# Recurrence gates of a hybrid decoder block as 64-row products on two halves of the array

## The chip, the cores and the metric

The kernel runs on one core of a Trainium2 chip. The time is the device time of one execution in microseconds (us). The kernel before took 1090.16 us, the median of three runs (1089.74 to 1090.64). The engines are named as in the profile: PE is TensorE (PEld its weight loads), DVE is VectorE, ACT is ScalarE, POOL is GpSimd, SP is the queue that starts most transfers. Each of them works off its own queue of instructions; semaphores tie the queues together.

## The reference

One decoder layer over 512 positions of 1024 channels. Three mixers work on the same normed input, their results are gated and merged, and a SwiGLU block follows. The change touches only the third mixer, a recurrence with 16 heads of 64 channels:

```python
def rglru_mixer(xr, gate, conv_w, conv_b, w_a, b_a, w_x, b_x, lam):
    xc = lax.conv_general_dilated(xr, conv_w[:, None, :], ...) + conv_b
    xh = xc.reshape(B, S, RNN_HEADS, RNN_HEAD_DIM)
    r = jax.nn.sigmoid(jnp.einsum('bshi,hio->bsho', xh, w_a).reshape(B, S, RNN_WIDTH) + b_a)
    i = jax.nn.sigmoid(jnp.einsum('bshi,hio->bsho', xh, w_x).reshape(B, S, RNN_WIDTH) + b_x)
    log_a = -LRU_C * r.astype(jnp.float32) * jax.nn.softplus(-lam.astype(jnp.float32))
    a = jnp.exp(log_a)
    b_in = jnp.sqrt(-jnp.expm1(2.0 * log_a)) * (i * xc).astype(jnp.float32)
    _, h = lax.associative_scan(combine, (a, b_in), axis=1)
    return h.astype(xr.dtype) * jax.nn.gelu(gate)
```

Each head has its own 64x64 matrix for the gate r (w_a) and for the gate i (w_x).

## The kernel before

All large products are made of 128x512 products of TensorE, with the channels on the partitions and the 512 positions along the free side. For precision every float32 operand is split in two parts, hi and lo (`split`, L130: ScalarE writes hi, VectorE writes lo as the rest), and a product of two operands becomes three: hi with hi, hi with lo, lo with hi. A tile (`matrix`, `passes`, L263) is 128 output channels: 8 blocks of input channels times three products, 24 products into one bank of PSUM. Its weights come in units of 512 KB; `unit` (L252) hands out the next one and starts the load and the split of the unit two tiles further on, into one of three buffers each for hi and lo.

The recurrence is done in two batches of four tiles (128 channels, so two heads, each). For a tile, `xr_tile`:

- makes the 24 products and adds the convolution: ScalarE writes xc from the bank (L499), VectorE adds three shifted terms (L501);
- splits xc into ch and cl (L131 on ScalarE, L136 on VectorE);
- makes both gates: the two 64x64 matrices of a tile lie on the diagonal of a 128x128 block of `wab`, with zeros beside them, so one gate is three 128x128 products into a bank of the tag "tr" (L509). ScalarE applies the sigmoid for r (L511) and a tanh for i (L514), and VectorE forms (tanh + 1) xc (L515).

`wab` is loaded and split early by `load_wab`, four splits of 512 elements per partition. After a batch, `rec_batch` makes the decay: a tanh of r per tile (L523), one square root over the four tiles (L524), exponentials (L530), each function set with a table load ahead of it, and then VectorE's scan (L542). The tiles `rg_tile` make the branch that the result is multiplied with, `gate_tile` (L712 to L724) the gates of another mixer, and `cmp_tile` a projection for it.

The order of the work: generators yield between pieces, and `run` draws them in turn. A tile that yields a number (`yield 4`) is put aside and drawn again that many yields later, so that its gates come out between the products of the next tile. A scheduler then sets the order on each engine; `tc.issue_after` makes an instruction stand behind another one. Banks of PSUM with the tag "mm" (six) and "tr" (two) are handed out in rotation.

Of the kernel before, what the change touches and what calls it, by code (L numbers as in the profile page):

```python
# [25 lines left out]
F32R = mybir.dt.float32r  # L26
I32 = mybir.dt.int32
AF = mybir.ActivationFunctionType
OP = mybir.AluOpType
# [23 lines left out]
def hybrid_block(ctx: ExitStack, tc: tile.TileContext, A, out):  # L53
# [61 lines left out]
    def bank(tag):  # L115
        return psum[1].tile([128, S], F32, tag=tag, name=nm(tag), bufs=psum[2][tag])
# [13 lines left out]
    def split(src, hi, lo, lo_eng=None):  # L130
        res["hi"] = SC.activation(hi, src, AF.Copy)  # L131
        e = lo_eng or V
        if e is GP:
            GP.tensor_sub(lo, src, f32(hi))
        else:
            res["lo"] = V.tensor_sub(lo, src, f32(hi))  # L136
# [318 lines left out]


    wab = {}

    def start_wab():
        wab["raw"] = slab("wabr", tag="s1", shape=(2, NK, 128))  # L460
# [2 lines left out]

    def load_wab():
        raw = wab["raw"]
        hi = slab("wabh", F32R, "wab", (2, NK, 128), 48)
        lo = slab("wabl", F32R, "wab", (2, NK, 128), 48)
        wab["hi"], wab["lo"] = hi, lo
        for _ in range(4):
            yield  # L470
        for k in range(0, NK, 2):
            split(raw[:, :, k:k + 2], hi[:, :, k:k + 2], lo[:, :, k:k + 2])
            yield

    yc = {}
    rec = {}
# [11 lines left out]
    def xr_tile(b, c):  # L488
# [11 lines left out]
        for i in (1, 2, 3):  # L500
            res["cv"] = V.scalar_tensor_tensor(xc[:, i:], ps[:, :S - i], cw(3 - i), xc[:, i:], op0=OP.mult, op1=OP.add)  # L501
        yield
        ch, cl = row("ch", F32R), row("cl", F32R)
        split(xc, ch, cl)
        yield 4
        for g, dst in ((0, "R"), (1, "TI")):
            pg = bank("tr")
            for t, (w, x) in enumerate((("hi", ch), ("hi", cl), ("lo", ch))):
                PE.matmul(pg, wab[w][:, g, k, :], x, start=(t == 0), stop=(t == 2))  # L509
            if g == 0:  # L510
                SC.activation(rec[b]["R"][:, c, :], pg, AF.Sigmoid, bias=vec[:, V_BA + k:V_BA + k + 1])  # L511
            else:
                ti = rec[b]["TI"][:, c, :]
                last = SC.activation(ti, pg, AF.Tanh, scale=0.5, bias=half[:, 0, k:k + 1])  # L514
                res["ti"] = last, V.scalar_tensor_tensor(ti, ti, 1.0, xc, op0=OP.add, op1=OP.mult)  # L515
            yield

    def rec_batch(b):
        r = rec[b]
        r["T"] = slab("t", tag="s2")  # L520
        for c in range(4):
            k = 4 * b + c
            SC.activation(r["T"][:, c, :], r["R"][:, c, :], AF.Tanh, scale=sp4[:, k:k + 1])  # L523
        root = SC.activation(r["T"], r["T"], AF.Sqrt, scale=1.0 / 16)  # L524

        def exps(cs):
# [1739 lines left out]
```

## Time and profile before

| | us |
|---|---|
| median of three runs | 1090.16 |
| the profiled execution | 1089.44 |
| its span, first to last instruction | 1087.7 |
| PE busy | 1078.3 |
| DVE busy | 883.0 |
| ACT busy | 661.7 |
| gate products (L509), first to last start | 66.8 to 143.6 |

The profile is of one execution. A row of a timeline has the start and the length in us, the engine, the line, the operation, its output and inputs, and in brackets the idle time of the engine ahead of it and what ended it. A row of a group has the count, the busy time, the mean duration in ns and the idle time ahead. A row of stretches has the time from and to, its length, the busy time of each engine (PE, PEld, DVE, ACT, POOL) with the number of instructions, the granted clock of TensorE (1.00 is full speed) and the share and rate of the transfers. Recorded products of TensorE overlap, so their durations add up to more than the time that they take.

### The profile page before, as it was taken

To read this page: it belongs to the slowest core of one execution; us is meant where nothing else is said; L and a number is where in the kernel's file an instruction comes from. 1 tells how busy PE (TensorE), PEld (TensorE's weight loads), DVE (VectorE), ACT (ScalarE), POOL (GpSimd) and SP (SyncE) were. 2 spreads that over 40 slices of the span, in tenths; PEclk is the share of its full clock that TensorE was granted. 3 is DMA by queue.
4 is the path that set the end of the run, shared out by engine and by line. 5 is a ranking of instruction groups with operands and counts; after the bars stand their busy time and mean duration, and the time that the engine had idled before them with its cause. 6 is when DMAs were issued, how large, how long until landed. Compare 5 with 4: busy or idle time off the path is not lost.

```text
span 1087.7 us, 16765 instructions
## 1 busy us (share of the span) xinstructions
PE 1078.3 (99%) x6450; PEld 948.5 (87%) x6450; DVE 883.0 (81%) x1557; ACT 661.7 (61%) x1210; POOL 29.0 (3%) x41
## 2 busy tenths in 40 slices
PE   9999999999999999999999999999999999999997
PEld 7888888999889888898888889988999999998886
DVE  6967779669675899998998887876988888889675
ACT  6757574454444676876777655555666666667542
POOL 0000000000000000000000000000000000022200
PEclk9999999999999999999999999999999999999999
DMA  8332325430322221102111134271323322378902
GB/s 312 113 99 82 97 86 204 178 98 20 117 78 78 78 59 39 59 20 79 59 39 59 58 118 136 72 257 39 117 78 117 117 104 97 130 227 202 191 20 97
DMA packets 35312, 115.07 MB, mean 106 GB/s; under 512 B 3584, under 2 KB 3984, under 8 KB 34336
## 3 DMA queue, kind: packets, MB, share of 16 engines
q1 hardware_dynamic: 28496, 97.01, 27.0%
q0 software_dynamic: 5152, 11.09, 5.0%
q10 hardware_dynamic: 1584, 5.90, 1.4%
q8 instruction: 50, 0.82, 0.3%
q14 instruction: 30, 0.25, 0.1%
HBM read 111.89 MB, written 2.10 MB: 105 GB/s over the span
## 4 chain that ended last, share of the span: by engine, by line
PE 97%; DVE 1%; DMA 0%; issue 0%; ACT 0%; DVEq 0%; SPq 0%; ACTq 0%
PE mm L263 37%; PE mm L1755 18%; PE mm L1273 7%; PE mm L1894 6%; PE mm L625 4%; PE mm L1509 4%; PE o L992 4%; PE sc L954 3%; PE tr L979 3%; PE tr L1894 3%; PE mm L870 2%; PE tr L784 1%; PE tr L509 1%; PE mm L1611 1%; PE tr L685 1%; PE tr L892 1%
## 5 line engine op out<-in xcount | busy, mean ns | idle before, releaser
L263 PE MATMUL mm<-hh,hi 128*128 128x512 f32 x504 | 199.5, 396 | 0.0
L263 PE MATMUL mm<-hh,lo 128*128 128x512 f32 x504 | 197.4, 392 | 0.0
L263 PE MATMUL mm<-hl,hi 128*128 128x512 f32 x504 | 196.9, 391 | 0.0
L136 DVE TENSOR_TENSOR lo<-raw,hi 128x1024 fp32r<-128x1024 f32 (+1 forms) x105 | 121.0, 1153 | 38.4 <-ACT hi L131 35.3
L131 ACT ACTIVATE hi<-raw 128x1024 fp32r<-128x1024 f32 (+1 forms) x105 | 105.3, 1003 | 46.5 <-PE mm L263 17.3
L263 PEld LDWEIGHTS mm<-hh,lo 128*128 128x128 f32 x504 | 94.6, 188 | 19.7
L263 PEld LDWEIGHTS mm<-hl,hi 128*128 128x128 f32 x504 | 94.7, 188 | 18.4 <-issue 0.2
L263 PEld LDWEIGHTS mm<-hh,hi 128*128 128x128 f32 x504 | 94.7, 188 | 18.0 <-PE mm L1273 0.2
L960 ACT ACTIVATE P<-P,ast 128x128 f32<-128x128 f32 (+3 forms) x128 | 70.7, 555 | 23.1 <-DVE ast L958 22.5
L958 DVE CUSTOM_DVE_ANT_0 P<-sc,mask 128x128 f32<-128x128 f32 (+3 forms) x128 | 57.9, 484 | 8.2 <-PE sc L954 7.3
L131 ACT ACTIVATE ph<-tr 128x512 fp32r<-128x512 f32 x80 | 46.9, 592 | 25.9 <-PE tr L979 24.0
L136 DVE TENSOR_TENSOR pl<-tr,ph 128x512 fp32r<-128x512 f32 x80 | 54.4, 685 | 2.7 <-PE o L992 0.9
L954 PE MATMUL sc<-K,q 128*128 128x512 f32 (+2 forms) x192 | 51.0, 368 | 0.0
L1755 PE MATMUL mm<-t,hi 128*128 128x256 f32 x288 | 50.7, 276 | 0.0
L1894 PE MATMUL mm<-hi,u 128*128 128x512 f32 x160 | 50.1, 389 | 0.0
L979 PE MATMUL tr<-ident,P 128*128 128x128 f32 x320 | 48.7, 273 | 0.0
L979 PEld LDWEIGHTS tr<-ident,P 128*128 128x128 f32 x320 | 39.0, 140 | 9.8 <-DVE pl L136 1.0
L136 DVE TENSOR_TENSOR lo<-bs,hi 128x1024 fp32r<-128x1024 f32 x28 | 34.1, 1220 | 11.6 <-ACT hi L131 11.6
L1755 PEld LDWEIGHTS mm<-t,hi 128*128 128x128 f32 x288 | 43.4, 188 | 0.0
L1755 PE MATMUL mm<-fh,hi 128*128 128x256 f32 x144 | 40.0, 278 | 0.0
L1755 PE MATMUL mm<-fh,lo 128*128 128x256 f32 x144 | 39.8, 276 | 0.0
L1755 PE MATMUL mm<-fl,hi 128*128 128x256 f32 x144 | 39.8, 276 | 0.0
(489 smaller groups left out, 2896.6 us busy)
## 6 DMA issues: line engine op xcount, KB each, us to landing
raw<-in_w_in SPq DMA_DIRECT2D x64, 512.0 KB, 3.5
rawp<-in_w_fi SPq DMA_DIRECT2D x20, 1024.0 KB, 5.1
bs<-in_w_fo POOLq DMA_DIRECT2D x20, 512.0 KB, 8.1
raw<-in_w_br SPq DMA_DIRECT2D x14, 512.0 KB, 3.6
w<-in_cw ACTq DMA_DIRECT2D x4, 1024.0 KB, 6.7
raw<-in_w_o SPq DMA_DIRECT2D x8, 512.0 KB, 4.1
bs<-in_w_fo SPq DMA_DIRECT2D x8, 512.0 KB, 8.0
raw<-in_w_v SPq DMA_DIRECT2D x6, 512.0 KB, 4.9
```

The costliest lines, as they stand in the source:

```text
L131: res["hi"] = SC.activation(hi, src, AF.Copy)
L136: res["lo"] = V.tensor_sub(lo, src, f32(hi))
L263: res["mm"] = PE.matmul(ps[:m, n0:n1], w[:, k * 128:k * 128 + m], x[k][:, n0:n1], start=(t == 0), stop=(t == 3 * NK - 1))
L625: res["mm"] = PE.matmul(b[c], x[k][:, c * 128:(c + 1) * 128], w[:, kk * 512:kk * 512 + 512], start=(k == 0 and t == 0), stop=(k == NK - 1 ...
L954: PE.matmul(ps[:, :w * n].rearrange("p (b n) -> p b n", b=w), lhs, K[:, i, brs[0]:brs[-1] + 1, :n], start=(i == 0), stop=(i == 1))
L958: V.tensor_tensor_reduce(out=t, in0=ps[:, b * n:b * n + n], in1=mask[0][:, S - n:], scale=-0.125, scalar=3.0e38, op0=OP.add, op1=OP.min, a ...
L960: SC.activation(t, t, AF.Exp, scale=-1.0, bias=st[:, 0, j, b:b + 1], accum_out=st[:, 1, j, b:b + 1])
L979: PE.transpose(pt[:, j * 128:(j + 1) * 128], self.part(j, br)[:, kt * 128:(kt + 1) * 128], ident)
L992: PE.matmul(po, VV[:, kt, g % 2, br].rearrange("p i d -> p (i d)"), x, start=(br == 0 and kt == 0 and t == 0), stop=(br == 1 and kt == a a ...
L1273: res["mm"] = PE.matmul(ps, u[:, k * 128:k * 128 + 128], v[:, k], start=(start and k == t == 0), stop=(k == 3 and t == 2), skip_group_chec ...
L1755: res["mm"] = PE.matmul(ps, w[:, k * 128:k * 128 + 128], x[:, k], start=(start and k == t == 0), stop=(k == 3 and t == 2), skip_group_chec ...
L1894: PE.matmul(ps, a, b, start=id(ps) not in begun, stop=i == len(ops) - 1, skip_group_check=True)
```

## The change

`load_wab` stores the gate weights without the zeros: for a tile and a head 64 rows and 128 columns, of which 64 belong to r and 64 to i. The first head of a tile lies on partitions 0 to 63, the second on 64 to 127. A gate product (now L519) has 64 rows: it takes one head's 64 channels and gives r and i of that head, 128 outputs, in one bank. `xr_tile` saves xc, ch and cl of the first tile of a pair and makes the products of two tiles together: four banks, now of the tag "mm", and 12 products, alternating between the lower and the upper rows, in an order set by `tc.issue_after`; hi with ch first, then lo with ch, then hi with cl. ch and cl move to other buffers (tags "tg" and "q32", two each). ScalarE applies its functions to 64 partitions at a time, four per tile (L524, L525). The tile yields 3 instead of 4 ahead of its gates. In `rec_batch` the four tanh (now L535) stand behind the last gate activation.

```diff
@@ -455,6 +455,7 @@
 
 
     wab = {}
+    ends = slice(0, 64), slice(64, 128)
 
     def start_wab():
         wab["raw"] = slab("wabr", tag="s1", shape=(2, NK, 128))
@@ -463,14 +464,16 @@
 
     def load_wab():
         raw = wab["raw"]
-        hi = slab("wabh", F32R, "wab", (2, NK, 128), 48)
-        lo = slab("wabl", F32R, "wab", (2, NK, 128), 48)
+        hi = slab("wabh", F32R, "wab", (NK, 128), 48)
+        lo = slab("wabl", F32R, "wab", (NK, 128), 48)
         wab["hi"], wab["lo"] = hi, lo
         for _ in range(4):
             yield
-        for k in range(0, NK, 2):
-            split(raw[:, :, k:k + 2], hi[:, :, k:k + 2], lo[:, :, k:k + 2])
-            yield
+        for o in ends:
+            for i in range(2):
+                g = slice(64 * i, 64 * i + 64)
+                split(raw[o, i, :, o], hi[o, :, g], lo[o, :, g])
+                yield
 
     yc = {}
     rec = {}
@@ -500,27 +503,36 @@
         for i in (1, 2, 3):
             res["cv"] = V.scalar_tensor_tensor(xc[:, i:], ps[:, :S - i], cw(3 - i), xc[:, i:], op0=OP.mult, op1=OP.add)
         yield
-        ch, cl = row("ch", F32R), row("cl", F32R)
+        ch, cl = row("ch", F32R, "tg"), row("cl", F32R, "q32")
         split(xc, ch, cl)
-        yield 4
-        for g, dst in ((0, "R"), (1, "TI")):
-            pg = bank("tr")
-            for t, (w, x) in enumerate((("hi", ch), ("hi", cl), ("lo", ch))):
-                PE.matmul(pg, wab[w][:, g, k, :], x, start=(t == 0), stop=(t == 2))
-            if g == 0:
-                SC.activation(rec[b]["R"][:, c, :], pg, AF.Sigmoid, bias=vec[:, V_BA + k:V_BA + k + 1])
-            else:
-                ti = rec[b]["TI"][:, c, :]
-                last = SC.activation(ti, pg, AF.Tanh, scale=0.5, bias=half[:, 0, k:k + 1])
-                res["ti"] = last, V.scalar_tensor_tensor(ti, ti, 1.0, xc, op0=OP.add, op1=OP.mult)
+        rec[b]["x"] = rec[b].get("x", []) + [(k, xc, ch, cl)]
+        yield 3
+        if c % 2 == 0:
+            return
+        two = rec[b].pop("x")
+        pg = [[bank("mm") for _ in ends] for _ in two]
+        for t in range(3):
+            for i, (k, xc, ch, cl) in enumerate(two):
+                w, x = (("hi", ch), ("lo", ch), ("hi", cl))[t]
+                for n, own in enumerate(ends):
+                    with tc.issue_after(res["gate"].ins) if t + i + n else nullcontext():
+                        res["gate"] = PE.matmul(pg[i][n], wab[w][own, k, :], x[own], start=(t == 0), stop=(t == 2))
+        yield
+        for i, (k, xc, ch, cl) in enumerate(two):
+            R, ti = (rec[b][n][:, k % 4, :] for n in ("R", "TI"))
+            for n, own in enumerate(ends):
+                SC.activation(R[own], pg[i][n][:64], AF.Sigmoid, bias=vec[own, V_BA + k:V_BA + k + 1])
+                last = SC.activation(ti[own], pg[i][n][64:], AF.Tanh, scale=0.5, bias=half[own, 0, k:k + 1])
+            res["ti"] = last, V.scalar_tensor_tensor(ti, ti, 1.0, xc, op0=OP.add, op1=OP.mult)
             yield
 
     def rec_batch(b):
         r = rec[b]
         r["T"] = slab("t", tag="s2")
-        for c in range(4):
-            k = 4 * b + c
-            SC.activation(r["T"][:, c, :], r["R"][:, c, :], AF.Tanh, scale=sp4[:, k:k + 1])
+        with tc.issue_after(res["ti"][0].ins):
+            for c in range(4):
+                k = 4 * b + c
+                SC.activation(r["T"][:, c, :], r["R"][:, c, :], AF.Tanh, scale=sp4[:, k:k + 1])
         root = SC.activation(r["T"], r["T"], AF.Sqrt, scale=1.0 / 16)
 
         def exps(cs):
```

The first place is the end of the second batch on PE, where the last xr tile (its bank is mm_183 before and after), its gates and the first rg tile of the second batch (mm_194) meet. Before:

```order
L263 MATMUL mm_194_1279<-hh_12_134,hi_176_1169 128x512
L509 MATMUL tr_192_1268<-ch_189_1258,wabh_75_529 128x512 [waits Activation_49]
L509 MATMUL tr_193_1273<-ch_189_1258,wabh_75_529 128x512
L263 MATMUL mm_194_1279<-hl_14_136,hi_176_1169 128x512
L263 MATMUL mm_194_1279<-hh_12_134,lo_177_1170 128x512
L263 MATMUL mm_194_1279<-hh_12_134,hi_176_1169 128x512
L263 MATMUL mm_194_1279<-hl_14_136,hi_176_1169 128x512
L263 MATMUL mm_194_1279<-hh_12_134,lo_177_1170 128x512
L509 MATMUL tr_192_1268<-cl_190_1259,wabh_75_529 128x512 [waits DVE_49]
L509 MATMUL tr_192_1268<-ch_189_1258,wabl_76_530 128x512
```

And with the change:

```order
L263 MATMUL mm_183_1229<-hh_12_134,lo_168_1127 128x512
L519 MATMUL mm_190_1269<-ch_181_1220,wabh_75_529 128x512 [waits PE_49,Activation_49]
L519 MATMUL mm_191_1270<-ch_181_1220,wabh_75_529 128x512 [waits PE_49]
L519 MATMUL mm_192_1271<-ch_188_1265,wabh_75_529 128x512 [waits PE_49,Activation_49]
L519 MATMUL mm_193_1272<-ch_188_1265,wabh_75_529 128x512 [waits DVE_49]
L519 MATMUL mm_190_1269<-ch_181_1220,wabl_76_530 128x512
L519 MATMUL mm_191_1270<-ch_181_1220,wabl_76_530 128x512
L519 MATMUL mm_192_1271<-ch_188_1265,wabl_76_530 128x512
L519 MATMUL mm_193_1272<-ch_188_1265,wabl_76_530 128x512
L519 MATMUL mm_190_1269<-cl_182_1221,wabh_75_529 128x512 [waits DVE_49]
L519 MATMUL mm_191_1270<-cl_182_1221,wabh_75_529 128x512
L519 MATMUL mm_192_1271<-cl_189_1266,wabh_75_529 128x512 [waits DVE_49]
```

Before, the first gate product of that tile stands behind 13 products of the rg tile, and six gate products of the tile ahead of it stand before those. Now the gates stand right behind the tile's own last product, those of the tile ahead (ch_181) in turn with its own (ch_188), and the whole rg tile stands behind the group. The group of the first batch's last two tiles stands behind the 16 products of `gate_tile`; the first group of each batch stands inside the third tile, behind 18 of its products.

The second place is ACT around the end of the first batch, where r and ti are the gates, t is the decay, hi the split of a weight unit. Before:

```order
L511 ACTIVATE r_86_631<-tr_128_860,vec_85 128x512
L523 ACTIVATE t_134_896<-r_86_631,sp4_96 128x512
L514 ACTIVATE ti_88_633<-tr_129_865,half_95 128x512
L524 ACT_TABLE_LOAD
L524 ACTIVATE t_134_896<-t_134_896 128x2048
L530 ACT_TABLE_LOAD
L530 ACTIVATE r_86_631<-r_86_631,spm8_97 128x512 x4
L451 ACTIVATE gs_135_912<-mm_130_871 128x512
L131 ACTIVATE hi_138_920<-raw_137_918 128x1024
```

And with the change:

```order
L524 ACTIVATE r_86_631<-mm_127_848,vec_85 64x512
L525 ACTIVATE ti_88_633<-mm_127_848,half_95 64x512
L524 ACTIVATE r_86_631<-mm_128_849,vec_85 64x512
L525 ACTIVATE ti_88_633<-mm_128_849,half_95 64x512
L535 ACTIVATE t_134_904<-r_86_631,sp4_96 128x512 x4
L451 ACTIVATE gs_135_920<-mm_130_879 128x512
L536 ACT_TABLE_LOAD
L536 ACTIVATE t_134_904<-t_134_904 128x2048
L542 ACT_TABLE_LOAD
L542 ACTIVATE r_86_631<-r_86_631,spm8_97 128x512 x4
L453 ACTIVATE gs_135_920<-gs_135_920 128x512
L131 ACTIVATE hi_138_928<-raw_137_926 128x1024
```

The tanh of the decay, one behind each tile's r before, are now four in a row behind the last gate, and the square root, the exponentials and the next split stand behind them. On DVE the lo of that split stands behind the first scan.

The third place is DVE at the last xr tile (mm_183). With the change:

```order
L136 TENSOR_TENSOR cl_182_1221<-xc_180_1210,ch_181_1220 128x512
L136 TENSOR_TENSOR lo_186_1233<-raw_184_1230,hi_185_1232 128x1024
L504 SCALAR_TENSOR_TENSOR xc_187_1260<-mm_183_1229,vec_85,xc_187_1260 128x511
L504 SCALAR_TENSOR_TENSOR xc_187_1260<-mm_183_1229,vec_85,xc_187_1260 128x510
L504 SCALAR_TENSOR_TENSOR xc_187_1260<-mm_183_1229,vec_85,xc_187_1260 128x509
L136 TENSOR_TENSOR lo_197_1299<-raw_195_1296,hi_196_1298 128x1024
L136 TENSOR_TENSOR cl_189_1266<-xc_187_1260,ch_188_1265 128x512
```

One weight split stands ahead of the three convolution steps, and one between them and cl; before, only the second did.

## The prediction

> **What bounds the kernel now.** I read the page first, then the chain of waits, then the timelines of the stretch that the change touches.
>
> ```profile
> span 1087.7 us, 16765 instructions
> PE 1078.3 (99%) x6450; PEld 948.5 (87%) x6450; DVE 883.0 (81%) x1557; ACT 661.7 (61%) x1210; POOL 29.0 (3%) x41
> PE 97%; DVE 1%; DMA 0%; issue 0%; ACT 0%; DVEq 0%; SPq 0%; ACTq 0%
> 125.00:147.00 22.00, 22.00 (x98) 18.06 (x97) 13.92 (x19) 14.81 (x22) 0.00 (x0) 1.00 0.32 96
> 180.00:215.00 35.00, 35.00 (x238) 31.84 (x236) 26.39 (x33) 14.90 (x25) 2.98 (x5) 1.00 0.49 178
> 215.00:345.00 130.00, 130.00 (x778) 115.07 (x777) 95.05 (x158) 59.85 (x97) 2.34 (x5) 1.00 0.27 83
> ```
>
> TensorE is the chain from end to end, and in the stretches by time it is busy for all of 125 to 147, 180 to 215 and 215 to 345 us. So a microsecond of TensorE time won or lost among the gates reaches the end unchanged. The price of a product is its slot, not its recorded duration, because products overlap:
>
> ```profile
> 132.34 1.36 PE tr L509 x6
> 133.70 5.44 PE mm L263 x24
> 139.14 1.36 PE tr L509 x6
> L509 PE MATMUL tr<-ch,wabh x16: 389/389/496, 66.8 to 143.6; 128*128 128x512 f32 x16
> ```
>
> Six gate products take 1.36 us of the chain, 0.2267 us each, though one is recorded with 389 ns. A tile of 24 products takes 5.44 us.
>
> **What is removed.** 48 products at L509, 12 to a pair of tiles. Afterwards 48 products again, of 64 rows, neighbours on opposite halves. If two halves run together, a group of 12 costs 6 slots, 1.36 us instead of 2.72: 5.44 us less over four groups. No row here shows such a pair, so this term has two ends: 6 slots, or 12 (no gain). The nearest rows are the one place that uses half the rows, against a full-height operation with as short a moving side:
>
> ```profile
> 87.71 0.32 PEld L722 LDWEIGHTS tr<-ident,gsig 64*128 64x128 f32 x4 [0.35 <-ACT gsig L718]
> 88.10 0.50 PE L509 MATMUL tr<-ch,wabh 128*128 128x512 f32 x1
> 88.43 0.39 PE L509 MATMUL tr<-cl,wabh 128*128 128x512 f32 x1
> 353.12 1.73 PE tr L892 x16
> L722 PEld LDWEIGHTS tr<-ident,gsig x4: 135/138/138, 87.7 to 87.9; 64*128 64x128 f32 x4
> ```
>
> Four half-height weight loads of 138 ns fill 0.32 us, so they start 0.06 us apart; full-height pairs of load and short product come 0.108 us apart (1.73/16). Two half-height loads fit into one slot of 0.2267, so loads do not forbid 6 slots, which I take. Going back to the full array, the next product was recorded 0.50 us instead of 0.39 and its successor came 0.33 us later instead of 0.2267: I price each change of height at 0.1 us, 0.2 a group, 0.8 in all (ends 0 and 0.16, the tail of 389 behind a slot of 227 ns).
>
> The Trainium skill, "TensorEngine Tiling (Array Packing)", Key Properties, says that a change of tiling mode drains the array; the 0.10 us above is what this trace shows of it. By its sister page "TensorE: Matmul & The Clock Gate", Part 3, products on different row groups run together, which is the 6-slot end; no run here shows it yet.
>
> **What is added on ScalarE.** Sixteen activations of 128 partitions become 32 of 64.
>
> ```profile
> L511 ACT ACTIVATE r<-tr,vec 128x512 f32<-128x512 f32 x8 | 5.5, 684 | 3.9 <-PE tr L509 3.9
> L716 ACT ACTIVATE gsig<-mm 64x512 f32<-64x512 f32 x1 | 0.6, 596 | 1.0 <-PE mm L712 1.0
> L451 ACT ACTIVATE gs<-mm 128x512 f32<-128x512 f32 x8 | 4.7, 584 | 2.3 <-PE mm L263 2.3
> 134.00 0.68 ACT L511 ACTIVATE r<-tr,vec 128x512 f32<-128x512 f32 x1
> 134.57 0.69 ACT L514 ACTIVATE ti<-tr,half 128x512 f32<-128x512 f32 x1
> ```
>
> Half the partitions save nothing (596 against 584 ns), and two such activations start 0.57 us apart. So 16 x 0.57 = 9.1 us more on ScalarE, eight in a row per group (4.6 us). ScalarE has the room on average; what counts is who queues behind them.
>
> **Where it lands: the wait for the second tile of a pair.** These rows follow the last xr tile of before, from its last product to its two operands:
>
> ```profile
> 138.75 0.39 PE L263 MATMUL mm<-hh,lo 128*128 128x512 f32 x1
> 139.18 0.78 ACT L499 ACTIVATE xc<-mm,vec 128x512 f32<-128x512 f32 x1 [2.79 <-PE mm L263]
> 139.99 2.32 DVE L501 SCALAR_TENSOR_TENSOR xc<-mm,vec,xc 128x511 f32<-128x511 f32 x3 [2.15 <-ACT xc L499]
> 142.56 0.64 ACT L131 ACTIVATE ch<-xc 128x512 fp32r<-128x512 f32 x1
> 142.83 1.22 DVE L136 TENSOR_TENSOR lo<-raw,hi 128x1024 fp32r<-128x1024 f32 x1
> 143.96 0.69 DVE L136 TENSOR_TENSOR cl<-xc,ch 128x512 fp32r<-128x512 f32 x1
> 143.28 0.69 PE L509 MATMUL tr<-ch,wabh 128*128 128x512 f32 x2
> 143.44 0.53 PE tr L509 x2
> ```
>
> From the start of the tile's last product, ch is ready 4.45 us later (142.56+0.64) and cl 5.90 later. Before, TensorE filled this with 19 other products (six gates of the tile ahead, 13 of the next rg tile), so the first ch product followed 4.53 us after that start. In the changed order the covers differ from group to group. "Slot 20" means that the product's turn comes 20 x 0.2267 us after that start.
>
> Groups one and three: 18 products of the next tile stand between, so the second tile's ch is wanted in slot 20, 4.53 us, and its cl in slot 24, 5.44. ScalarE has no gate activations ahead of them yet: xc begins 0.42 us after the last product's start, the convolution ends at 3.56, ch at 4.3, and cl follows a small split at about 5.0 in group one, a whole weight split (1.22) at about 5.3 in group three. No wait.
>
> Group two: the 16 products of the branch-gate tile and one pair stand between: slot 18, 4.08 us. Here the eight activations of group one, with the next xc among them, have pushed back one weight split; its lo ends on VectorE 1.9 us after the last product's start, and the convolution (2.32) stands behind it, so it ends at 4.15 instead of 3.56. Then ScalarE does the branch gates' copy (0.50) before ch (0.64): ch at 5.2. TensorE waits 1.15. cl, at 5.9 behind another split, is in time for its slot after that wait.
>
> Group four: nothing but one pair stands between: slot 2, 0.45 us. xc waits for a split's hi on ScalarE (0.15 later than above), the convolution for that split's lo (0.3 more): ch at 4.9, wait 4.45. The last cl comes at 5.9 and is wanted four slots after ch, 5.8: 0.1 more. The rg tile that covered this before stands behind the group on the same queue.
>
> **The sum.** Pair of groups one and two: 4 x 1.36 = 5.44 before; 2 x 1.36 + 0.4 + 1.15 = 4.27 after, 1.17 won. But the decay tanh stood between the gates and now follow them, with 0.57-us activations ahead:
>
> ```profile
> 90.44 0.67 ACT L514 ACTIVATE ti<-tr,half 128x512 f32<-128x512 f32 x1
> 92.42 1.92 ACT L524 ACTIVATE t<-t 128x2048 f32<-128x2048 f32 x1
> 96.40 1.30 DVE L539 SCALAR_TENSOR_TENSOR t<-r,t 128x512 f32<-128x512 f32 x2 [4.56 <-ACT r L530]
> 98.59 1.05 ACT L131 ACTIVATE hi<-raw 128x1024 fp32r<-128x1024 f32 x1
> 100.55 1.20 DVE L136 TENSOR_TENSOR lo<-raw,hi 128x1024 fp32r<-128x1024 f32 x1
> 104.07 0.39 PE L263 MATMUL mm<-hh,lo 128*128 128x512 f32 x1
> ```
>
> Group two ends near 85.3 us. Behind it on ScalarE stand eight gate activations and the branch sigmoid (9 x 0.57), four tanh (4 x 0.61) and one square (0.48), then a table load of 1.3: the square root starts near 94.65 instead of 92.42, and all behind it is 2.2 later. The lo of the fourth rg tile ends at 100.55+1.20+2.2 = 103.95; TensorE wants it at 104.07-1.17 = 102.9 and waits, with one product of the next tile put into the gap (0.23). Of 1.17 about 0.3 stays.
>
> Groups three and four: 5.44 before; 2.72 + 0.4 + 4.45 + 0.1 = 7.67 after, 2.2 lost. Net 1.9 later.
>
> **The clock.** A wait of over 4 us is new to this stretch. The only one as long is at the end:
>
> ```profile
> 1080.09 0.28 PE L2045 MATMUL mm<-hi,fs 128*128 128x256 f32 x1
> 1083.00:1083.20 0.20, 0.00 (x0) 0.00 (x0) 0.17 (x2) 0.00 (x0) 0.00 (x0) 1.00 0.00 0
> 1083.20:1083.40 0.20, 0.00 (x0) 0.00 (x0) 0.16 (x2) 0.00 (x0) 0.00 (x0) 0.59 0.17 41
> ```
>
> 2.9 us after the last product ended (1080.37) the granted clock falls. A 4.45-us wait passes that. What it costs is between 0 (it does not fall there) and 1.4 us (it takes as long to come back as it took to fall, 2.9 us at half speed); neither end has a nearer row, so I take the middle, 0.7.
>
> The Trainium skill, "TensorE: Matmul & The Clock Gate", Part 1, has the clock halve after a whole free-running window of about 3.4 us without work; by that it falls in some executions and not in others, and the sum would be 1.9 or some 3.3.
>
> The sum: 1.9 + 0.7 = 2.6 us. The profiled execution took 1089.44 with a span of 1087.7; 2.6 makes 1092.0 with a span near 1090.3. The median is 0.72 above the profiled one: **1092.7 us**. Behind group four the same chain of eight activations, four tanh, square root and exponentials stands ahead of the lo of the last rg tile, which TensorE wants three tiles (16.3 us) after the group; by the durations above it comes 0.2 to 0.7 us before that, so I add nothing. The splits of the gate weights cost nothing: four of 512 elements before and after, well before 66.8 us, under a busy TensorE; were they late, the first group would wait, 0.7 us for each.
>
> **The rivals.**
> *The waits are filled.* If the order of the queues did not bind, or ch came sooner, the gain would be 5.44 - 0.8 = 4.6 us: 1085.5. For it: the operations exist and ScalarE is 61% busy. Against: the gap of 0.35 us at L722 above, with ready products behind it, shows that TensorE does not pass a waiting instruction. Partly true (the fourth wait 2 us shorter, no clock loss): 1090.1, no change.
> *No clock loss:* the forecast's lower end, 1092.1, within 0.2%.
> *The halves do not run together,* so the change does not do what it says: from 12 slots on. The groups cost 2.72 each. One and two then lose the change of height and the wait (0.4 + 0.9, a slot more of cover), and the lo about 0.5 more, since ScalarE's chain has moved with them; three and four lose 2.2 + 2.7 - 0.2 = 4.7. Together 6.5, 1096.6. For it: no such pair in the trace; against: the half-height loads above.
>
> **How the numbers follow.** Forecast (long wait in group four) 0.58, own range 1091.8 to 1094.0; waits filled 0.18; partly 0.14; halves apart 0.10. What a measurement tells from no change is about 0.2%, 2.2 us. The forecast's range crosses that bound at 1092.3: two thirds of it lie above. Slower: these (0.39) and the halves apart, 0.49. Same: the other third (0.19), most of partly (0.10), a little of filled (0.02): 0.31. Faster: 0.20, the rest. The range leaves out the fastest tenth and the slowest tenth: 1088.5 to 1095.5.
>
> **What would show it.** Gate products in pairs, six slots a group: 6-slot end right. A TensorE gap of 4 to 5 us after the last xr tile, ended by ScalarE's ch: group four right; of about 1.1 after the branch-gate tile: group two. The fourth rg tile's third product released by VectorE's lo near 104 us. Granted clock below 1 near 142 to 146 us: the clock term. I am wrong if TensorE passes the waiting gate, or if ch comes within 2 us.

## The result

The changed kernel took 1103.81 us, the median of four runs (1103.18 to 1105.07), against 1090.40 for the kernel before (1089.74 to 1091.14): a ratio of 1.0124, 95% interval 1.0107 to 1.0142. The forecast was 1092.7 with a range up to 1095.5. The direction was right, the size was not: 13.4 us were lost instead of 2.3.

The profiled execution took 1103.27 us, 13.83 more than the one of before. Two lines of its page, the engines and the chain's shares:

```profile
PE 1080.5 (98%) x6450; PEld 945.7 (86%) x6450; DVE 884.2 (80%) x1557; ACT 675.7 (61%) x1226; POOL 29.0 (3%) x41
PE 87%; DVE 5%; ACT 4%; DMA 3%; issue 1%; DVEq 0%; SPq 0%; ACTq 0%
```

The chain was 97% TensorE; now 12% of it belongs to VectorE, ScalarE and a transfer. TensorE's busy time, 1080.5 us, is no guide here: it contains products at half clock, and idle time is what was added.

The pairs do what the change says. The timeline of TensorE through group one, and the chain's piece for it:

```profile
70.50 0.39 PE L263 MATMUL mm<-hh,lo 128*128 128x512 f32 x1
70.82 0.73 PE L519 MATMUL mm<-ch,wabh 64*128 64x512 f32 x4
71.38 0.62 PE L519 MATMUL mm<-ch,wabl 64*128 64x512 f32 x4
71.84 0.62 PE L519 MATMUL mm<-cl,wabh 64*128 64x512 f32 x4
72.40 0.50 PE L263 MATMUL mm<-hh,hi 128*128 128x512 f32 x1
72.73 0.39 PE L263 MATMUL mm<-hl,hi 128*128 128x512 f32 x1
70.89 1.58 PE mm L519 x12
```

Four products, two pairs, start 0.46 us ahead of the next four (71.38 to 71.84): 0.23 a pair, one slot. Twelve take 1.58, in group three too, where the kernel before needed 2.72.

And this is where TensorE then stands still (timeline; the bracket is the idle time and what ended it):

```profile
84.92 0.50 PE L519 MATMUL mm<-ch,wabh 64*128 64x512 f32 x2 [1.40 <-ACT ch L131]
87.80 0.46 PE L734 MATMUL tr<-ident,gsig 64*128 64x64 f32 x4 [0.47 <-ACT gsig L730]
104.51 0.50 PE L263 MATMUL mm<-hh,hi 128*128 128x512 f32 x1 [0.37 <-ACT hi L131]
105.94 0.50 PE L263 MATMUL mm<-hh,hi 128*128 128x512 f32 x1 [0.69 <-ACT hi L131]
106.59 0.50 PE L263 MATMUL mm<-hh,lo 128*128 128x512 f32 x1 [0.16 <-DVE lo L136]
140.94 0.51 PE L519 MATMUL mm<-ch,wabh 64*128 64x512 f32 x2 [0.29 <-ACT ch L131]
146.10 0.80 PE L519 MATMUL mm<-ch,wabh 64*128 64x512 f32 x2 [4.65 <-ACT ch L131]
149.12 0.63 PE L263 MATMUL mm<-hl,hi 128*128 128x512 f32 x1
149.54 0.63 PE L263 MATMUL mm<-hh,lo 128*128 128x512 f32 x1
188.35 2.05 PE L796 MATMUL tr<-x,w 128*128 128x124 f32 x16 [0.36 <-DVE x L777]
337.09 0.50 PE L263 MATMUL mm<-hh,hi 128*128 128x512 f32 x1 [3.27 <-DVE u L454]
```

Group four waits 4.65 us, as forecast, and then runs slowly: products at 149.12 and 149.54 start 0.42 us apart instead of 0.2267. The last row is the surprise: 3.27 us at 337 us, far from the gates, between the last u tile and the first q tile of the next phase. The stretches by time around both waits (the last four numbers are POOL, the granted clock, the transfers' share and rate):

```profile
144.00:147.40 3.40, 1.30 (x6) 1.11 (x8) 3.02 (x4) 0.63 (x1) 0.00 (x0) 0.50 0.49 154
147.40:150.80 3.40, 3.40 (x11) 2.20 (x10) 0.00 (x0) 2.53 (x4) 0.00 (x0) 0.50 0.83 231
338.00:342.00 4.00, 4.00 (x13) 3.13 (x11) 1.11 (x2) 0.63 (x1) 0.57 (x2) 0.57 0.01 4
```

The clock is at half for 6.8 us around the first wait, most of it spent on work, and for 3.4 us behind the second.

Start times of the same product in both traces give the balance. A wait costs some 0.2 us more than its bracket, since the product ahead of it is recorded with 0.39 and has a slot of 0.2267.

| place | forecast, us | measured, us |
|---|---|---|
| 48 products at half the slots | -5.4 | -5.4 |
| changes of height, four groups | +0.8 | +1.6 |
| group two: wait, and the branch gates' transposes behind it | +1.15 | +2.2 |
| weights of the fourth rg tile and of the one behind it | +0.9 | +2.0 |
| group four: waits on ch | +4.5 | +5.3 |
| half clock behind it | +0.7 | +2.1 |
| input of the compression | 0 | +0.6 |
| from the u tiles to the q tiles | 0 | +5.1 |
| sum | +2.6 | +13.5 |

The remaining 0.3 of the 13.83 is not assigned.

### The profile page after: what moved, and what is told of

Same layout as the page of the kernel before. It is cut to its first block, busy times and chain, and to the rows that moved or that the text cites. A ratio compares the mean times of both kernels' runs of the same rounds, so it can differ in the third digit from the quotient of the medians.

```text
span 1101.6 us, 16803 instructions
## 1 busy us (share of the span) xinstructions
PE 1080.5 (98%) x6450; PEld 945.7 (86%) x6450; DVE 884.2 (80%) x1557; ACT 675.7 (61%) x1226; POOL 29.0 (3%) x41
## 4 chain that ended last, share of the span: by engine, by line
PE 87%; DVE 5%; ACT 4%; DMA 3%; issue 1%; DVEq 0%; SPq 0%; ACTq 0%
PE mm L263 31%; PE mm L1767 17%; PE mm L1285 7%; PE mm L1906 6%; PE mm L637 4%; PE o L1004 4%; PE sc L966 3%; PE tr L991 3%; PE tr L1906 3%; PE mm L882 2%; PE mm L1521 2%; PE tr L796 1%; DMA raw<-in_w_o 1%; DVE lo L136 1%; PE mm L1623 1%; DMA raw<-in_w_in 1%
```

## The experiments

Each run is compared with runs of the kernel before on the same chip; their medians lay between 1089.7 and 1090.2. The changed kernels themselves ran on different chips in part; where two of them are compared, the difference of their ratios stands beside the difference of their times.

### The rotation of the banks

In the program as built the first q tile of the next phase takes bank 0. The last u tile had bank 3 before; in the changed kernel it has bank 0, because the gates now take 16 more tiles from the "mm" rotation. Then the first q product must wait until VectorE has read the last u tile (L454). One write into a fresh bank ahead of the u tiles moves the rotation on by one, in either kernel:

```diff
+    V.memset(bank("mm")[:, :8], 0.0)
     run([u_tile(j) for j in range(8)])
```

> The kernel before with one small write of zeros into a fresh "mm" bank on VectorE (8 columns, nobody reads them) right ahead of the u tiles, so that the PSUM banks are handed out one further: the last u tile and the first q tile of the next phase then share a bank, as they do in the changed kernel. Nothing of the gates is touched. Theory (the 5.1 us lost between the u tiles and the q tiles come from the rotation of the banks, by a wait of about 3.3 us for the evacuation of the last u tile and a lower clock behind it): +5.1 us, near 1095.5. Rival (the loss there follows from the lateness of the stages ahead): no change, 1090.4, within 1 us.

> The changed kernel with the same one small write ahead of the u tiles, which moves its rotation on by one, so that the last u tile has another bank than the first q tile. Theory (bank rotation): 5.1 us less than the changed kernel, near 1098.7, and no wait of the first q product on VectorE's u. Rival (lateness): 1103.8, the wait stays.

The kernel before with the other rotation took 1095.68 us (ratio 1.0051, 1.0034 to 1.0068), 5.9 more, and its trace has the same wait, with the clock at half for 6.8 us around it (part of that in the second row):

```profile
328.77 0.80 PE L263 MATMUL mm<-hh,hi 128*128 128x512 f32 x1 [3.27 <-DVE u L454]
328.00:331.00 3.00, 2.23 (x5) 1.83 (x6) 2.24 (x4) 0.63 (x1) 0.82 (x2) 0.50 0.44 153
```

The changed kernel with the rotation put right took 1097.84 (ratio 1.0074, 1.0059 to 1.0089): 6.0 less than 1103.81, or 5.5 by the two ratios. Its trace has no such wait; TensorE is busy all through the stretch in which the first q product starts (334.2 us):

```profile
332.00:336.00 4.00, 4.00 (x23) 3.42 (x23) 2.91 (x4) 2.18 (x3) 0.00 (x0) 1.00 0.03 12
```

So some 40% of the loss has nothing to do with the gates' work: it comes from which bank comes next. The lateness of the stages ahead plays no part. The four runs of the first of the two kernels also show that the clock does not fall in every execution: they lie from 1093.39, with a mean granted clock of 0.999, to 1097.03 with 0.995. The fastest is 3.6 us above before, the bare wait with its refilling; the others pay for the clock as well.

### Group four: the wait and the clock

Sixteen products that nobody reads, put into the wait:

```diff
                 for n, own in enumerate(ends):
+                if b and c == 3 and t == 0 and i == 0:
+                    idle = bank("tr")
+                    for _ in range(16):
+                        with tc.issue_after(res["gate"].ins):
+                            res["gate"] = PE.matmul(idle, wab["hi"][:, k, :], two[0][2], start=True, stop=True)
```

> The changed kernel with 16 products added between the first and the second tile's pairs of group four, into a bank that nobody reads: 3.6 us of work inside the wait of 4.65 us. Theory (the wait lets the granted clock fall to half, which costs 2.4 us after the wait has ended): the clock stays at 1, 2.4 us less than the changed kernel, near 1101.4, although 16 products are added. Rival (the slow products behind the wait are slow because of the half-height pairs, not because TensorE had idled): they stay slow, 1103.8.

The real cover, the rg tile ahead of group four instead of behind it:

```diff
-    run(four(rg_tile, 0) + [cmp_tile(1)] + tiles[:4], rec_batch(0), 0.45)
+    run(four(rg_tile, 0) + [cmp_tile(1)] + tiles[:5], rec_batch(0), 0.45)
...
-    run([tiles[4], *(rg_tile(1, c) for c in range(1, 4)), cmp_tile(2), inputs(cmp_tile(3), 0),
+    run([*(rg_tile(1, c) for c in range(1, 4)), cmp_tile(2), inputs(cmp_tile(3), 0),
```

> The changed kernel with the rg tile that stands behind group four put ahead of it in the queue of the main tiles, so that 18 of its products stand between the last xr tile and the second tile's pairs, as in groups one and three. Theory (group four loses its 5.5 us by its bare wait and the clock behind it): the wait goes to under 0.5 us, the clock stays at 1, and the time falls by 4.5 to 7 us, to 1097 to 1099. Rival (the wait is set by ScalarE's eight activations in a row, whatever stands in TensorE's queue): less than 2 us of gain, over 1101.8.

Both runs did what they were made for, and neither won the time. The filled kernel took 1103.10 (ratio 1.0123, 1.0108 to 1.0138), the covered one 1103.06 (1.0121, 1.0106 to 1.0137), against 1.0124 for the changed kernel. First the filled one, then the covered one:

```profile
146.10 0.51 PE L519 MATMUL mm<-ch,wabh 64*128 64x512 f32 x2 [0.79 <-ACT ch L131]
146.00:150.00 4.00, 3.90 (x21) 2.92 (x22) 1.06 (x2) 2.49 (x5) 0.00 (x0) 1.00 0.65 214
165.32 0.50 PE L263 MATMUL mm<-hh,lo 128*128 128x512 f32 x1 [0.71 <-DVE lo L136]
188.13 2.05 PE L801 MATMUL tr<-x,w 128*128 128x124 f32 x16 [1.21 <-DVE x L782]
```

```profile
167.43 0.52 PE L263 MATMUL mm<-hh,hi 128*128 128x512 f32 x1 [1.86 <-ACT hi L131]
169.02 0.80 PE L263 MATMUL mm<-hh,lo 128*128 128x512 f32 x1 [0.64 <-DVE lo L136]
171.00:174.00 3.00, 3.00 (x9) 2.32 (x8) 3.00 (x6) 2.33 (x5) 0.00 (x0) 0.50 0.80 304
```

In the filled kernel the clock stays at 1.00 through 146 to 150 us: it was the idleness, not the half-height products, that made them slow there. But what TensorE gains there it loses at 165 us, where the lo of a later tile's weights is late, and at 188 us, at the compression's input. In the covered kernel group four has no wait of its own any more; 20 us later TensorE waits 1.86 and 0.64 us for the weights of the last rg tile, and the clock falls there instead. By the starts of the same products the covered kernel is 6.7 us ahead of the changed one at 150 us, 0.8 at 175 and 0.2 at 190. The expected gains of 2.4 and of 4.5 to 7 us were given back within 45 us. ScalarE's chain (eight activations, four tanh, root, exponentials, then hi) is a second bound, just behind TensorE; the wait of group four had hidden it.

### ScalarE's part alone

The kernel before, with each gate activation split in two, the tanh of the other gate like this sigmoid:

```diff
-                SC.activation(rec[b]["R"][:, c, :], pg, AF.Sigmoid, bias=vec[:, V_BA + k:V_BA + k + 1])
+                for o in (slice(0, 64), slice(64, 128)):
+                    SC.activation(rec[b]["R"][o, c, :], pg[o], AF.Sigmoid, bias=vec[o, V_BA + k:V_BA + k + 1])
```

> The kernel before with each of its 16 gate activations given as two of 64 partitions; its products stay full-height. This is the ScalarE part of the change alone. In the changed kernel such activations start 0.705 us apart, against 0.57 us for 128 partitions before. Theory (it is the 64-partition form that comes 0.705 us apart, and the 13.5 us more on ScalarE make the weights behind it late): spacing near 0.7 us, and 0.5 to 3 us longer than before, 1090.3 to 1093. Rival (the spacing comes from results that are written to other partitions than they are read from, which this kernel does not do, and ScalarE has room): spacing 0.57 us, no change, 1089.8.

It took 1091.64 (ratio 1.0018, 1.0009 to 1.0028): slower by 1.9 us, with full-height products. Rows of ScalarE's timeline:

```profile
136.53 0.68 ACT L516 ACTIVATE ti<-tr,half 64x512 f32<-64x512 f32 x1
137.12 0.62 ACT L131 ACTIVATE ch<-xc 128x512 fp32r<-128x512 f32 x1
141.49 1.37 ACT L512 ACTIVATE r<-tr,vec 64x512 f32<-64x512 f32 x2
142.88 0.69 ACT L516 ACTIVATE ti<-tr,half 64x512 f32<-64x512 f32 x1
```

Two halves take 1.39 us from start to start (141.49 to 142.88), 0.695 each, though here each half is read from and written to the same partitions. So the move to other partitions is not needed for the 0.70 us. Half height by itself does not force it either: the split of ch starts 0.59 us behind a half-height tanh (136.53 to 137.12), before that has ended. What keeps two half-height gate activations in succession from overlapping is not shown.

### Do the halves run together?

The changed kernel with the loop over the halves outermost, so six products of one half and then six of the other:

```diff
+        for n, own in enumerate(ends):
             for t in range(3):
                 for i, (k, xc, ch, cl) in enumerate(two):
-                for n, own in enumerate(ends):
```

> The changed kernel with the 12 products of a group in another order: the six of one half, then the six of the other, so that neighbours stand on the same rows of the array save once. Theory (two products of 64 rows run together only as neighbours on different halves): 11 slots instead of 6 in a group, 2.5 us for 1.36, about 1.1 us more for each of four groups, and up to 2.3 in group four where the clock is at half: 1107 to 1110, less what later slack takes. Rival (a product of 64 rows takes half a slot by itself): no change, 1103.8.

```profile
70.87 0.72 PE L519 MATMUL mm<-ch,wabh 64*128 64x512 f32 x2
71.44 0.39 PE L519 MATMUL mm<-ch,wabl 64*128 64x512 f32 x1
71.54 0.49 PE L519 MATMUL mm<-ch,wabh 64*128 64x512 f32 x1
71.66 0.39 PE L519 MATMUL mm<-ch,wabl 64*128 64x512 f32 x1
73.11 0.50 PE L263 MATMUL mm<-hh,hi 128*128 128x512 f32 x1
```

Group one takes 2.24 us (first row to the next tile's product) and group three, by the same reading, 2.54, against 1.58. A product of 64 rows costs a full slot unless its neighbour is on the other half; the rival falls. Group one is below the expected 2.5 because the second half does not wait for the first: at 71.54 a product of the second half starts between the third and the fourth of the first. The whole time, 1100.69 (ratio 1.0097, 1.0082 to 1.0112), was below the expected 1107 for a reason that the expectation did not contain: the other order of release gave the last u tile bank 3, and the wait at the phase change was gone. Against the changed kernel with its rotation put right it is 2.9 us slower, 2.5 by the ratios; some of that is the clock, which is at half for 13.7 us among the gates here and for 6.8 there.

### The place of the tanh, and cover for every group

Without the rule that queues the decay tanh behind the gates (rotation put right):

```diff
-        with tc.issue_after(res["ti"][0].ins):
-            for c in range(4):
+        for c in range(4):
```

> The changed kernel with the rotation put right by the small write (as in the second experiment, 1097.8) and without the rule that queues the decay tanh behind the gates: two of each four then stand ahead of the second tile's gates, as early as their sigmoids allow. Theory (the eight 64-partition activations make the weights late, not the place of the tanh): 1096.5 to 1098.5, since what the weights gain group two loses by a tanh ahead of its ch. Rival (the place of the tanh makes the weights late): the waits for hi and lo vanish and 2 us or more are won, under 1096.

It took 1096.63 (ratio 1.0060, 1.0043 to 1.0077), 1.2 less than with the rule, 1.5 by the ratios, whose intervals overlap. The waits for the fourth rg tile's weights did vanish, as the rival had it. It expected 2 us or more from that; the two traced executions differ by 2.0, the medians by less. The bare wait of group four (4.66 us) and its half clock remain. Group two's wait stayed at 1.40, so the theory's price for the tanh there was wrong.

Then cover for every group, on top of that:

```diff
-        yield 3
+        yield 4
...
-    run(xr_tiles(0, gate_tile()))
-    run(four(rg_tile, 0) + [cmp_tile(1)] + tiles[:4], rec_batch(0), 0.45)
+    first_rg = rg_tile(0, 0)
+    run(xr_tiles(0, gate_tile()) + [first_rg])
+    run([*(rg_tile(0, c) for c in range(1, 4)), cmp_tile(1)] + tiles[:5], rec_batch(0), 0.45)
```

> As the run beside it (rotation put right, tanh free), and every group's pairs stand one step of six products later, with the next rg tile ahead of groups two and four, so that 24 products (5.4 us), or the branch gates' 16 and what follows, stand between an xr tile and its pairs. Theory (the bare waits of groups two and four, and the clock behind the second, are the loss that is left): waits on ch under 0.5 us in all, clock at 1, 1088.5 to 1092. Rival (the weights of later tiles come late by ScalarE's chain and their wait takes the place of the one removed, as when group four alone was covered): 1094 to 1098.

```profile
85.42 0.50 PE L519 MATMUL mm<-ch,wabh 64*128 64x512 f32 x2 [2.12 <-ACT ch L131]
85.94:89.35 3.41, 3.41 (x15) 2.15 (x14) 2.51 (x5) 3.08 (x6) 0.00 (x0) 0.50 0.52 181
185.93 2.05 PE L795 MATMUL tr<-x,w 128*128 128x124 f32 x16 [2.68 <-DVE x L776]
```

It took 1095.02 (1.0046, 1.0029 to 1.0063). Group four is free. Group two is not: it now waits 2.12 us, and in the profiled execution that alone sends the clock to half for 3.4 us. And the compression's input has become the longest wait: its buffer is that of the decays (tag "s2"), so it waits for the last scan, and the scans for ScalarE's exponentials.

The runs from here on move the order alone. Group two two steps later, the first batch's tanh behind its gates again, and the scans ahead of the branch outputs:

```diff
-        yield 4
+        yield 4 if b or c < 3 else 6
...
+        with nullcontext() if b else tc.issue_after(res["ti"][0].ins):
...
-        yield from after(res["ti"], rec_out(0))
         yield from batch
+        yield from after(res["ti"], rec_out(0))
```

> As the run that covered every group (1095.0), with three moves of the order: group two's pairs stand two steps (12 products, 2.7 us) later; the decay tanh of the first batch are behind its gates again; and in the run of the second batch its scans are recorded ahead of the first batch's branch outputs, because the compression input that TensorE waited 2.68 us for reuses the buffer of the decays and so waits for the last scan. Theory (group two's wait of 2.12 us with 1.7 us of half clock behind it, and the compression input's 2.68 us, are most of what is left of the loss): both waits under 0.5 us, 1088 to 1090.5. Rival (ScalarE's longer chain moves the wait on to the next late weights or scans): 1092 to 1095.

The same with the side work recorded more slowly, so that hi comes ahead of the root:

```diff
-        both_out(), 0.45)
+        both_out(), 0.3)
```

> As the run beside it, with the side work of the last stretch (root, exponentials, scans, branch outputs) recorded at 0.30 of a step for each step of the main tiles instead of 0.45, which puts the hi of two weights ahead of the root on ScalarE. Theory (the weights' waits of about 1.1 us near 164 us come from the chain of tanh, root and exponentials ahead of their hi): those waits vanish, and the compression input comes later by one or two operations on VectorE; within 1 us of the run beside it, 1087.5 to 1091. Rival (the scans are the binding chain): the compression input's wait grows by 2 us or more, over 1091.

They took 1092.33 (1.0019, 1.0009 to 1.0029) and 1093.43 (1.0034, 1.0022 to 1.0046). In the first, waits of 1.24, 1.35, 1.06 and 1.46 us are left, 5.1 in all against 5.9 in the kernel with every group covered; in the second the 1.06 us for weights are gone, the compression waits 2.48, and the sum is 5.6. The rivals have it, a wait removed comes back at the next place, though the compression's wait grew by 1.0 us and not by the 2 that the second rival asked for. The two orders were then joined, with the branch gates' transposes three steps later (the second of the two kernels has 3 and 0.8 in the last places):

```diff
-        exps((0, 1) if b else range(4))
+        exps((0, 1))
...
         SC.activation(s[:64], s[:64], AF.Sigmoid)
-        yield
+        yield 4
...
-    run([*(rg_tile(0, c) for c in range(1, 4)), cmp_tile(1)] + tiles[:5], rec_batch(0), 0.45)
+    run([*(rg_tile(0, c) for c in range(1, 4)), cmp_tile(1)] + tiles[:5], rec_batch(0), 0.3)
...
+        for _ in range(2):
+            yield 1
         batch = rec_batch(1)
...
-        both_out(), 0.45)
+        both_out(), 0.6)
```

> As the run with the branch outputs put back (1092.3), whose waits left were 1.24 us at the branch gates' transposes, 1.35 and 1.06 us for weights and 1.46 us for the compression input, 5.1 us in all, each with some 0.2 us of refilling behind it. Moves of the order alone: the branch gates' transposes three steps later; the weights' hi ahead of the root on ScalarE in both batches (side work recorded at 0.30 for the first, begun two steps later and then at 0.60 for the second), the first batch's exponentials in two pairs. Theory (what is left of the change, 3.8 us less work on TensorE with a height change priced by its rows at 0.42 us a group, shows once these waits are gone): 1087 to 1089.5, faster than before by up to 0.3%. Rival (ScalarE and VectorE have too little slack for 13.5 us more of activations, so the waits move on): 1090 or more.

> The same with the second batch's side work begun three steps later and then recorded at 0.80 of a step: its scans stand closer together on VectorE, ahead of the copies of the compression tiles. Theory (the compression input is set by the last scan): its wait is under 0.5 us, and the time within 0.7 us of the run beside it. Rival: as there, 1090 or more.

They took 1092.11 (1.0014, 1.0005 to 1.0024) and 1090.22 (1.0002, 0.9993 to 1.0010). Both fit the rival (1090 or more), and the compression's wait, which the second was to bring under 0.5 us, is the one wait of size that is left in both. First the one, then the other, each with the clock around it:

```profile
180.97 3.63 PE L796 MATMUL tr<-x,w 128*128 128x124 f32 x16 [2.97 <-DVE x L777]
177.49:180.91 3.42, 0.51 (x3) 0.09 (x1) 3.33 (x5) 0.76 (x1) 0.00 (x0) 1.00 0.51 153
180.91:184.32 3.41, 3.35 (x15) 3.35 (x16) 3.41 (x7) 0.89 (x2) 0.72 (x1) 0.50 0.04 5
```

```profile
181.10 2.05 PE L796 MATMUL tr<-x,w 128*128 128x124 f32 x16 [2.73 <-DVE x L777]
175.98:179.39 3.41, 2.39 (x11) 1.49 (x9) 3.35 (x7) 0.60 (x1) 0.00 (x0) 1.00 0.22 36
179.39:182.81 3.42, 1.71 (x15) 1.72 (x16) 3.39 (x5) 1.58 (x2) 0.00 (x0) 1.00 0.29 117
```

In the profiled executions 2.97 us of waiting halve the clock and 2.73 at the same place do not. The traces suggest why. The clock changes only on a grid of 3.41 us that runs through an execution: in the changed kernel it changes at 144.0, 150.8, 338.6 and 342.0 us, which lie 2, 55 and 1 steps apart. The first wait lies almost whole in one step, with 2.9 us idle (the first stretch above); the second is cut by the grid into 1.02 and 1.71 us. The last two runs put one gate tile's 24 products ahead of the compression, to see whether this wait is the rest of the loss; the first kernel's edit is shown, the second has `c_gate(1), inputs(hidden(first), 1)` in that place and the other line untouched:

```diff
-         behind(c_gate(0), "x0", "x1"), hidden(first), inputs(c_gate(1), 1)],
+         behind(c_gate(0), "x0", "x1"), c_gate(1), hidden(first), inputs(c_gate(2), 1)],
...
-        run([c_gate(2), hidden(second), c_gate(3)], begin(), 1.5)
+        run([c_gate(3), hidden(second)], begin(), 1.5)
```

> As the last run of the order (1090.2, where one wait of 2.73 us for the compression input was left), with the next gate tile's 24 products put ahead of the compression's products, and the one after that ahead of the second compression's inputs: 4.5 us more of work between. Theory (that wait is the last place where the saving of the pairs goes): no wait there, 2.7 to 2.9 us less, 1087.2 to 1088, faster than before by 0.2 to 0.3%. Rival (the second compression or the sums behind it have lost their cover): a new wait of 1 us or more at their products, 1088.5 to 1091.

> The same with only the one gate tile moved ahead of the first compression, so that the second keeps more of its cover behind it. Theory: as there, 1087.2 to 1088. Rival: a wait of 1 us or more at the second compression, whose input has 31 products (7 us) ahead of it instead of 44, 1088.5 to 1091.

```profile
211.51 0.38 PE L1285 MATMUL mm<-ych,hi 128*128 128x256 f32 x1 [0.89 <-ACT hi L131]
212.30 0.51 PE L1285 MATMUL mm<-t,hi 128*128 128x256 f32 x2 [0.29 <-ACT r L1289]
215.52 0.38 PE L1285 MATMUL mm<-ych,hi 128*128 128x256 f32 x1 [0.36 <-ACT r L1293]
```

They took 1090.11 and 1090.17 (both 1.0001, 0.9992 to 1.0010). The compression's wait is gone, and three waits on ScalarE of 1.54 us in all (rows of the first kernel) stand some 30 us later. The theory of a last wait falls for good. By the starts of the same products the first of these kernels is 2.5 us ahead of the kernel before at 175 us and 0.6 behind at 240. So the saving of the pairs is real, and it is handed back: those three waits with their refilling are 2.1 of the 3.1 us, the rest is not assigned. With every long wait covered, the half-height gates equal the kernel before and do not beat it. Whether fewer operations on ScalarE would free the rest was not tried.

## Why the prediction was right and wrong

**Six slots for a group: right.** The choice between the two ends was the half-height weight loads 0.06 us apart, and the pairs run together. The rival of halves apart falls twice, by the chain's 1.58 us and by the run that separates them.

**The change of height: half its price.** The step took two changes of 0.1 us from the row at L722. The starts in group one show four places: 0.09 ahead of the first pair, 0.11 more between the first two fours (0.56 for two slots of 0.2267), 0.11 ahead of the first full product and 0.10 behind it. That is 0.41 a group, and a group saves 0.95 us, not 1.16.

**Group two: right place, too short.** Forecast 1.15, measured 1.40 by its bracket and 1.7 with the refilling. The eight activations ahead of ch were priced at 0.57 us each, from full-height rows. The chain shows:

```profile
74.87 0.68 ACT r L524
75.57 0.69 ACT ti L525
80.69 1.23 DVE lo L136
81.94 3.49 DMA raw<-in_w_in
85.46 1.06 ACT hi L131
97.21 1.92 ACT t L536
```

They start 0.70 us apart, so eight take 5.6 and not 4.6. The row of half height that the prediction quoted, 0.596 us for one, gave the length of a single operation; no row showed two in succession, and the step took the spacing of another form. A second thing was left out, and it falls on the next term: the next transfer of raw weights starts when the lo of the ones before is made (80.69 + 1.23 against 81.94 above), so a late hi, with its lo behind it, delays the transfer too, and until 85.46 ScalarE stood at a hi whose data had just landed, with the gates' activations behind it.

**The lo of the fourth rg tile: right mechanism, too small by 1 us,** for the same 0.14 us times eight and the late transfer: the root began at 97.21, where the forecast had 94.65. Most of the waiting was for two hi of ScalarE (0.37 and 0.69 us), 0.16 for the lo.

**Group four: right.** 4.45 forecast, 4.65 measured. The 5.3 of the table has 0.29 more, a wait for the first tile's ch that the sum did not have, and the refilling.

**The clock: right mechanism, its upper bound too low.** The bounds were 0 and 1.4 us, from a fall 2.9 us after the last product and a return that takes as long. The clock was at half for two lengths of 3.4 us, of which 4.7 us (146.10 to 150.82) were spent on work: 2.1 us by the starts. The step that failed here is the upper bound: the return took longer than the fall. By the Trainium skill, "TensorE: Matmul & The Clock Gate", Part 1, the clock changes in windows of about 3.4 us; the stretches of half clock here, 3.4 and 6.8 us, agree. The same section of the Trainium skill says that the clock falls after a window without work; here 2.12 us of idle time were enough (the kernel with every group covered), and the measurement decides.

**"Behind group four ... so I add nothing": wrong as a statement of slack.** In the changed kernel that chain cost only 0.6 us, because TensorE was itself 8 us late. The covered kernel shows that it is short by 2.5 us (waits of 1.86 and 0.64) the moment TensorE is on time: the step left 0.2 to 0.7 us of slack, from activations priced at 0.57 us.

**What no step contained: the banks.** That the gates' banks move from "tr" to "mm" stands in the description of the change; the prediction does not mention it and counts nothing for it. It followed who waits for the gates, not who inherits the rotation 200 us later. This term, put at nothing without a reason, is the step that failed most: the runs show 5.1 us for it, of the 11.2 by which the sum was too small. It is not all: with the rotation put right the changed kernel still took 1097.84, above the 1095.5 at which the range ended. The other parts are terms of the sum that were too small: the half clock by 1.4, the weights by 1.1, group two by 1.0, group four and the changes of height by 0.8 each, and the compression's input, put at nothing, by 0.6.

## What to carry to other kernels

Count what a change takes from a rotation of buffers, and look at the end of that rotation: a shift by some tiles can put a reader and a writer on one bank at a phase change far away, and the same shift costs or saves time in a kernel that otherwise stays as it was. Before pricing a wait that is removed, find the slack of the second engine in the chain; here cover for group four brought nothing that could be measured until other places had cover as well. And price an operation in its new shape from two of them in succession.

## What the hardware showed unexpectedly

- The stretches of half clock last whole multiples of 3.4 us: 3.4 behind a wait of 2.12, 6.8 behind 4.65. They begin and end on one grid of such steps, and what decides seems to be the idle time of TensorE within a single step. In the traces here the clock fell behind every step with 1.86 us of idle time or more (1.86 in the covered kernel) and behind none with 1.83 or less (1.83 in the kernel with the slower side work), up to the last product. There is one exception: in the kernel that works off one half after the other it fell at 88.1 us, behind a step with 0.5 us of idle time that holds a group of half-height products. This is read off the traces, no run was made for it.
- So the same wait can cost nothing, one step or two: the 3.27 us at the phase change gave 3.4 us of half clock in the changed kernel and 6.8 in the kernel before with the other rotation, whose four runs have mean clocks from 0.999 to 0.995.
- Two halves of the array work off their products as two streams: in the kernel with one half after the other, a product of the second half (71.54) started between the third and the fourth of the first, although all six of the first stand ahead of it in the queue.
- Two half-height gate activations in succession start 0.70 us apart on ScalarE, two full-height ones 0.57: there half the partitions cost more, not the same.
